# A half step's third weight sum in the raw ring, and the operand sums transposed ahead into two pairs of PSUM banks

## The chip, the cores and the metric

One core of one Trainium2 chip runs the whole program. The metric is the device time of one execution in microseconds (us), taken as the median of several runs; lower is better. TensorE is called PE here, its weight load PEld, VectorE DVE, ScalarE ACT, GpSimd POOL and the queue of SyncE, which issues the weight loads, SP.

## The reference

The kernel computes two transformer layers on one sequence of 512 tokens of width 1024 in fp32. Layer 0 mixes tokens by two kinds of attention, layer 1 by a pool mixer; behind each stands a feed-forward network. What matters for this change is that network and its sandwich norms (hidden width 2816 = 22 columns of 128, that is 11 column pairs):

```
h = h + rmsnorm(mixer(rmsnorm(h)))
u = rmsnorm(h)
h = h + rmsnorm((silu(u @ w_gate) * (u @ w_up)) @ w_down)
```

## The kernel before, in words

**Precision.** PE takes fp32r operands, so each fp32 matrix is split into a high part and a low part (hi, lo), and a product is three matmuls: hi·hi, hi·lo, lo·hi (`three` at L332 to L334, `prod` at L944 to L946). Weights come from HBM into a ring of raw tiles (`load_raw`, tag `wr`, 11 tiles of 128x512, DMAs on the SP queue); `conv` makes the high part on ACT (L244, tile `wh`) and the low part on DVE or POOL (L245, tile `wl`) in a second ring, `wq`, of 14 tiles, which are 7 hi/lo pairs.

**The feed-forward network.** `Ffn.run` computes gate and up of the 11 column pairs in 22 half steps. A half step is a 2x2 block product with seven block products in place of eight. Each has 4 x 3 = 12 matmuls of 256 columns: `begin` does the products of weights "11" and "s2" into a psA bank, `middle` "s3" and "s1" into a psS bank and then "12" into psA, `end` "22" and "s4" into psS. Two of the seven (p1 from "11" and "12") are already there for the column pairs that `front` computed ahead, so their half steps have five. The weight sums s1 to s4 of a half step are made on DVE by `comb` in `pair_weights` (L913): a half step loads four raw tiles (a11, a21, a22, a12), s3 = a11 - a21 goes into a tile of its own, and the other three sums overwrite raw tiles (a21, a11, a12). s3's tile comes from a ring of two tiles, tag `jk`, which it shares with the products `mq` of `post_norm` (L822). `put` then converts each block into hi and lo.

**The operand sums.** `combine` makes the four sums of blocks of the normed activations (tiles `tt`, L881, on DVE) and transposes each on PE, two times four 128x128 transposes per sum (`transpose_pair`, L311). Each group of four lands in one PSUM bank of tag psT, of which there are two; ACT takes the high part (L220, tile `th`), DVE the low part (L221, tile `tl`), and then the bank is free. `turn` transposes the normed activations themselves (tiles `un` into `uh` and `ul`) the same way. The tags psA, psS, psT and psO have two banks each.

**What sets the order.** A scheduler puts each engine's instructions in a fixed order when the kernel is built, by program order, priorities and its own estimate of time; `tc.high_priority(n)` puts its body ahead by n places. `conv` and `comb` run with n = `hpw` = 0. On the chip every engine works through its own list in order, so an instruction that has to wait holds all behind it. Between the attention or the pool mixer and `run` stand transition 1 (around 280 to 360 us) and transition 2 (640 to 740 us), whose program order is a string of steps: W and T are products of the projection before, N, E and F the norms, M the mixer, R `turn`, A `front`, Z `combine`. In both strings Z stands second to last, ahead of one A alone.

Of the kernel before, what the change touches and what calls it, by code (L numbers as in the profile page):

```python
# [6 lines left out]
F32 = mybir.dt.float32  # L7
# [6 lines left out]
P = 128  # L14
# [15 lines left out]
CFG = dict(  # L30
    order=ORDER,
    norm='vggvgvvg',
    wlo0='g',
    wlo1='ggv',
    ng=31,
    no=8,
    xe=4,
    pt=4,
    w=14,
    wr=11,  # L40
    jk=2,
    psb=(2, 2, 2, 2),
    early=('kc', 'vc'),
# [9 lines left out]
    hpa=200,  # L53
# [59 lines left out]
def trunk(ctx: ExitStack, tc, x, norm_g, w_in, b_f, cmp_pe, cmp_w1, cmp_w2, w_out,  # L113
# [9 lines left out]
    def nm(s):  # L123
        names[s] = names.get(s, 0) + 1
        return f"{s}_{names[s]}"

    def T(shape, tag, bufs, dt=F32, label=None):
        return sb.tile(shape, dt, tag=tag, bufs=bufs, name=nm(label or tag))
# [3 lines left out]
    def G(shape, dt=F32, label="g"):  # L132
        return T(shape, "g", CFG["ng"], dt, label)
# [7 lines left out]
    def JK(label, n=S, dt=F32):  # L141
        return T([P, n], "jk", CFG["jk"], dt, label)
# [13 lines left out]
    def BANK(tag, shape=(P, S)):  # L156
        return ps.tile(list(shape), F32, tag=tag, bufs=psb[tag], name=nm(tag))

    def r32(ap):
        return ap.bitcast(F32)  # L160
# [4 lines left out]
    def cols(w, c0, n, k0=0, nk=KC):  # L165
        return w[k0 * P:(k0 + nk) * P, c0:c0 + n].rearrange("(k p) f -> p k f", p=P)

    def load_raw(src, shape):

        n, w = shape[1:]  # L170
        m = max(1, min(n, 512 // w))
        raws = []
        for a in range(0, n, m):
            raw = T([P, m, w], "wr", CFG["wr"])
            nc.sync.dma_start(raw, src[:, a:a + m, :])
            raws.append(raw)
        return raws
# [41 lines left out]
    def split(dst_hi, dst_lo, src):  # L219
        nc.scalar.activation(dst_hi, src, AF.Copy)  # L220
        nc.vector.tensor_sub(dst_lo, src, r32(dst_hi))  # L221
# [4 lines left out]
    def WQ2(shape):  # L226
        return WQ(shape, "wh"), WQ(shape, "wl")
# [11 lines left out]
    def next_engine(key):  # L239
        return nc.vector if choose(key) == "v" else nc.gpsimd  # L240

    def conv(hi, lo, src, key="wlo"):
        with tc.high_priority(CFG["hpw"]):
            nc.scalar.activation(hi, src, AF.Copy)  # L244
            next_engine(key).tensor_tensor(lo, src, r32(hi), op=ALU.subtract)  # L245
# [60 lines left out]
    def transpose_pair(dst, srcs, ks, tag, gcol=None):  # L306

        pt = BANK(tag)
        for a, k in enumerate(ks):
            for j in range(2):  # L310
                nc.tensor.transpose(pt[:, a * 256 + j * P:a * 256 + (j + 1) * P], srcs[j][:, k * P:(k + 1) * P], ident)  # L311
        hi, lo = dst
        if gcol is None:
            split(hi, lo, pt.rearrange("p (k c) -> p k c", k=2))
            return
        for a, k in enumerate(ks):
            g = gT[:, gcol * 8 + k:gcol * 8 + k + 1]
            o = pt[:, a * 256:(a + 1) * 256]
            nc.scalar.activation(hi[:, a, :], o, AF.Copy, scale=g)
            nc.vector.scalar_tensor_tensor(lo[:, a, :], o, g, r32(hi[:, a, :]), op0=ALU.mult, op1=ALU.subtract)  # L320
# [4 lines left out]
    def transpose_half(u, uns, half, gcol=None, tags=("psT",), first=0):  # L325
        cs = slice(half * 256, (half + 1) * 256)
        for k2 in range(first, KC // 2):
            ks = slice(2 * k2, 2 * k2 + 2)
            transpose_pair((u[0][:, ks, cs], u[1][:, ks, cs]), uns, (2 * k2, 2 * k2 + 1), tags[k2 % len(tags)], gcol)
# [485 lines left out]
    def post_norm(t, bk, hs, g_bc, store=False):  # L815
        sq = SM([P, 2], "sq2")
        for n in range(2):
            nc.scalar.activation(trash[:, 0:S], bk[n], AF.Square, scale=1.0 / 32, accum_out=sq[:, n:n + 1])
        rs = rstd_of(sq)
        junk = [JK("mq") for _ in range(2)]  # L820
        for n in range(2):
            nc.vector.tensor_tensor(junk[n], bk[n], g_bc[n], op=ALU.mult)  # L822
        for n in range(2):
            cs = slice(n * S, (n + 1) * S)
            if choose("hup") == "v":
                nc.vector.scalar_tensor_tensor(hs[t][:, cs], junk[n], rs, hs[t][:, cs], op0=ALU.mult, op1=ALU.add)
            else:
                nc.scalar.activation(junk[n], junk[n], AF.Copy, scale=rs)
                nc.gpsimd.tensor_tensor(hs[t][:, cs], junk[n], hs[t][:, cs], op=ALU.add)
            if store:  # L830
                (nc.sync, nc.scalar)[n].dma_start(out[0, t * P:(t + 1) * P, cs], hs[t][:, cs])
# [4 lines left out]
    class Ffn:  # L836
# [14 lines left out]
            self.uns.append(norm_row(self.hs[t], self.g))  # L851

        def turn(self, half):
            transpose_half(self.u, self.uns[2 * half:2 * half + 2], half, first=2 * half)

        def front(self, p):
            a = [RAW(2 * p), RAW(2 * p + 1)]
# [14 lines left out]
        def combine(self):  # L872

            lo_, hi_ = slice(0, S), slice(S, D)
            ts = [[], [], [], []]
            for j in range(2):
                a, b = self.uns[j], self.uns[2 + j]
                t1, t2, t3, t4 = (G([P, S], label="tt") for _ in range(4))
                for o, x0, x1 in ((t1, b[:, lo_], a[:, lo_]), (t3, b[:, hi_], b[:, lo_]),
                                  (t2, b[:, hi_], t1), (t4, a[:, hi_], t2)):  # L880
                    next_engine("sadd").tensor_tensor(o, x0, x1, op=ALU.subtract)  # L881
                for m, t_ in enumerate((t1, t2, t3, t4)):
                    ts[m].append(t_)
            self.T = {}
            for n_, m in enumerate((0, 2, 3, 1)):
                his, los = [], []
                for k2 in range(2):
                    hi, lo = (G([P, 2, 256], F32R, label=l_) for l_ in ("th", "tl"))
                    transpose_pair((hi, lo), ts[m], (2 * k2, 2 * k2 + 1), "psT")
                    his += [hi[:, k, :] for k in range(2)]  # L890
                    los += [lo[:, k, :] for k in range(2)]
                self.T[m + 1] = (his, los)
# [4 lines left out]
        def pair_weights(self, w_, p):  # L897


            def block(r, j):  # L900
                return load_raw(cols(w_, (2 * p + r) * P, P, 4 * j, 4), [P, 4, P])[0]

            a11, a21, a22, a12 = block(0, 0), block(1, 0), block(1, 1), block(0, 1)
            W = {}

            def put(name, src):
                hi, lo = WQ2([P, 4, P])
                conv(hi, lo, src, "slo")
                W[name] = ([hi[:, k, :] for k in range(4)], [lo[:, k, :] for k in range(4)])

            def comb(o, x0, x1, op):
                with tc.high_priority(CFG["hpw"]):
                    next_engine("sadd").tensor_tensor(o, x0, x1, op=op)  # L913

            s3 = JK("s3").rearrange("p (k c) -> p k c", k=4)
            if p not in self.ws:
                put("11", a11)
            comb(s3, a11, a21, ALU.subtract)
            comb(a21, a21, a22, ALU.add)
            comb(a11, a21, a11, ALU.subtract)  # L920
            put("s2", a11)
            yield W
            put("s3", s3)
            put("s1", a21)
            if p not in self.ws:
                put("12", a12)
            comb(a12, a12, a11, ALU.subtract)
            yield W
            put("22", a22)
            put("s4", a12)  # L930
            yield W
# [104 lines left out]
    f0 = Ffn(0, hs, G)  # L1036
# [12 lines left out]
        return  # L1049
    bk = {}  # L1050

    def post_feed(t):
        post_norm(t, bk[t], hs, g_bc)
        f0.feed(t)

    steps = {
        "T": lambda t: bk.__setitem__(t, tail(t)),
        "W": f0.weights,
        "N": post_feed,
        "R": f0.turn,  # L1060
        "A": f0.front,
        "Z": f0.combine,
    }
    for step in CFG["tr1"].split():
        steps[step[0]](*(int(c) for c in step[1:]))
# [2 lines left out]
    class Pool:  # L1068
# [82 lines left out]
    f1 = Ffn(1, hs, G)  # L1151
# [7 lines left out]
        "F": f1.feed,  # L1159
        "R": f1.turn,  # L1160
        "A": f1.front,
        "Z": f1.combine,
    }
    for step in CFG["tr2"].split():
        steps[step[0]](*(int(c) for c in step[1:]))
# [34 lines left out]
```

## Time and profile before

| what | value |
|---|---|
| median of 3 runs | 1073.12 us (1072.94 to 1074.51) |
| the profiled execution, its own time | 1071.16 us |
| its span, first to last instruction | 1069.4 us |
| mean granted clock of PE | 0.987 of 2.4 GHz |
| busy: PE, DVE, ACT, POOL | 96%, 71%, 53%, 29% of the span |
| HBM | 102 MB read, 97 GB/s over the span |

An engine's busy share is its time in instructions over the span. The granted clock is told as a share of full speed; a stretch at 0.52 is one at the lower of the two levels for nearly all of its time. Names such as `psT L311 <- DVE tl L221` say that the instruction of line 311 that writes psT waited for the instruction of line 221 on DVE that writes tl.

### The profile page before, as it was taken

The numbers are of one execution on the slowest core, as the hardware profiler recorded it, in microseconds if no ns is written. First come the engines' busy times: TensorE is split into PE (matmuls) and PEld (weight loads), VectorE is DVE, ScalarE is ACT, GpSimd is POOL, SyncE is SP. The second block draws the span as 40 slices with busy tenths as digits, with TensorE's granted clock in tenths as the row PEclk, the third lists the DMA queues.
The fourth block names the chain that finished last, engine by engine and source line by source line (L and its number), as shares of the span: only waits on it lengthen the run. The fifth ranks groups of instructions, "written<-read, shape, count | busy, mean of one in ns | idle before, by whom it ended". The sixth has DMA issues, their size and how long they took to land.

```text
span 1069.4 us, 19004 instructions
## 1 busy us (share of the span) xinstructions
PE 1023.3 (96%) x6892; PEld 940.4 (88%) x6892; DVE 755.3 (71%) x1527; ACT 563.0 (53%) x1194; POOL 314.5 (29%) x282
## 2 busy tenths in 40 slices
PE   6999999997999999999999999988999999999997
PEld 5788978896888999999988888988999999978886
DVE  5338898758749999899973153998898898881204
ACT  6437688769656454454564352764444354472401
POOL 5713666767751000000026371420000000053510
PEclk9999999999999999999999999998999999999999
DMA  8841201323531434433343374003342333433302
GB/s 244 195 96 40 60 21 32 95 73 102 169 89 31 119 109 116 123 102 107 119 153 114 106 218 110 21 11 92 97 138 83 112 114 90 139 117 121 108 1 78
DMA packets 156493, 108.58 MB, mean 102 GB/s; under 512 B 14836, under 2 KB 137584, under 8 KB 156400
## 3 DMA queue, kind: packets, MB, share of 16 engines
q1 hardware_dynamic: 155600, 106.23, 34.6%
q8 instruction: 54, 0.88, 0.4%
q10 hardware_dynamic: 800, 1.15, 0.3%
q14 instruction: 39, 0.32, 0.1%
HBM read 101.88 MB, written 2.10 MB: 97 GB/s over the span
## 4 chain that ended last, share of the span: by engine, by line
PE 77%; DVE 8%; ACT 5%; issue 3%; DMA 3%; POOL 2%; SPq 1%; DVEq 0%; POOLq 0%; ACTq 0%
PE psS L944 8%; PE psS L945 8%; PE psS L946 7%; PE psA L944 5%; PE psA L945 5%; PE psA L946 5%; PE psT L784 2%; PE psO L784 2%; PE psT L782 2%; PE psT L783 2%; PE psO L783 2%; PE psO L782 2%; PE psA L782 2%; PE psA L784 2%; PE psA L783 2%
## 5 line engine op out<-in xcount | busy, mean ns | idle before, releaser
L244 ACT ACTIVATE wh<-wr 128x512 fp32r<-128x512 f32 x376 | 226.3, 626 | 256.8 <-DVE wr L913 82.4
L245 POOL TENSOR_TENSOR wl<-wr,wh 128x512 fp32r<-128x512 f32 x101 | 145.4, 1449 | 556.5 <-ACT wh L244 329.8
L245 DVE TENSOR_TENSOR wl<-wr,wh 128x512 fp32r<-128x512 f32 x275 | 189.5, 706 | 92.1 <-ACT wh L244 89.4
L944 PE MATMUL psS<-th,wh 128*128 128x256 f32 x528 | 149.8, 285 | 1.3 <-DVE comb L964 1.3
L945 PE MATMUL psS<-tl,wh 128*128 128x256 f32 x528 | 150.0, 285 | 0.0
L946 PE MATMUL psS<-th,wl 128*128 128x256 f32 x528 | 149.9, 284 | 0.0
L944 PEld LDWEIGHTS psS<-th,wh 128*128 128x128 f32 x528 | 101.6, 193 | 1.6 <-DVE comb L964 0.9
L945 PEld LDWEIGHTS psS<-tl,wh 128*128 128x128 f32 x528 | 101.8, 193 | 0.0
L946 PEld LDWEIGHTS psS<-th,wl 128*128 128x128 f32 x528 | 101.7, 193 | 0.0
L913 DVE TENSOR_TENSOR wr<-wr,wr 128x512 f32<-128x512 f32 x132 | 86.7, 682 | 1.3 <-DMA wr<-in_ffn_w_up_dram 0.5
L946 PE MATMUL psA<-uh,wl 128*128 128x256 f32 x272 | 77.5, 286 | 3.1 <-DVE wl L245 3.0
L944 PE MATMUL psA<-uh,wh 128*128 128x256 f32 x272 | 77.5, 286 | 2.1 <-DVE comb L962 1.7
L945 PE MATMUL psA<-ul,wh 128*128 128x256 f32 x272 | 77.3, 284 | 0.0
L270 POOL TENSOR_SCALAR E<-E,ri 128x128 f32<-128x128 f32 (+3 forms) x48 | 56.0, 1167 | 38.8 <-DVE ri L590 12.9
L584 ACT ACTIVATE E<-E,mn 128x128 f32<-128x128 f32 (+1 forms) x96 | 53.4, 557 | 15.7 <-DVE mn L582 15.0
L946 PEld LDWEIGHTS psA<-uh,wl 128*128 128x128 f32 x272 | 52.6, 194 | 3.5 <-DVE wl L245 3.5
L944 PEld LDWEIGHTS psA<-uh,wh 128*128 128x128 f32 x272 | 52.5, 193 | 2.7 <-DVE comb L962 2.1
L332 PE MATMUL psA<-uh,wh 128*128 128x512 f32 (+1 forms) x136 | 51.4, 378 | 1.7 <-DVE nq L464 1.5
L945 PEld LDWEIGHTS psA<-ul,wh 128*128 128x128 f32 x272 | 52.6, 193 | 0.0
L221 DVE TENSOR_TENSOR pl<-psT,ph 128x512 fp32r<-128x512 f32 (+1 forms) x72 | 42.3, 593 | 12.5 <-ACT ph L220 8.7
L334 PE MATMUL psA<-uh,wl 128*128 128x512 f32 (+1 forms) x136 | 50.9, 374 | 0.0
L333 PE MATMUL psA<-ul,wh 128*128 128x512 f32 (+1 forms) x136 | 50.7, 373 | 0.0
(354 smaller groups left out, 3009.8 us busy)
## 6 DMA issues: line engine op xcount, KB each, us to landing
wr<-in_ffn_w_gate_dram SPq DMA_DIRECT2D x98, 256.0 KB
wr<-in_ffn_w_up_dram SPq DMA_DIRECT2D x98, 256.0 KB
wr<-in_ffn_w_down_dram SPq DMA_DIRECT2D x88, 256.0 KB
wr<-in_attn_w_in_dram SPq DMA_DIRECT2D x40, 256.0 KB
wr<-in_attn_w_out_dram SPq DMA_DIRECT2D x16, 256.0 KB
x<-in_x_dram SPq DMA_DIRECT2D x4, 512.0 KB
gbc<-in_norm_g_dram SPq DMA_DIRECT2D x8, 256.0 KB
h<-in_x_dram SPq DMA_DIRECT2D x4, 512.0 KB
```

The source lines that it names most:

```text
L244: nc.scalar.activation(hi, src, AF.Copy)
L245: next_engine(key).tensor_tensor(lo, src, r32(hi), op=ALU.subtract)
L270: (nc.vector if k == "v" else nc.gpsimd).tensor_scalar(e, e, s1, None, op0=ALU.mult)
L332: nc.tensor.matmul(psum, wh, ah, start=first, stop=False)
L584: nc.scalar.activation(e, e, AF.Exp, bias=mn[:, n_:n_ + 1], scale=-1.0, accum_out=sm[:, n_:n_ + 1])
L782: nc.tensor.matmul(o, acts[c][0][:, tok], wh[k], start=first, stop=False)
L783: nc.tensor.matmul(o, acts[c][0][:, tok], wl[k], start=False, stop=False)
L784: nc.tensor.matmul(o, acts[c][1][:, tok], wh[k], start=False, stop=last)
L913: next_engine("sadd").tensor_tensor(o, x0, x1, op=op)
L944: nc.tensor.matmul(o, wh, bh, start=start and k == 0, stop=False, skip_group_check=True)
L945: nc.tensor.matmul(o, wh, bl, start=False, stop=False, skip_group_check=True)
L946: nc.tensor.matmul(o, wl, bh, start=False, stop=k == 3, skip_group_check=True)
```

## The change

Four edits. The raw ring gets a twelfth tile. The sum s3 takes its tile from that ring and no more from `jk`. `turn` of the second half, and `combine`, put their groups of four transposes into psT and psO banks in turn. And `combine` runs with a priority 200 places ahead (`hpa` = 200) in both transitions.

```
-    wr=11,
+    wr=12,
...
         def turn(self, half):
-            transpose_half(self.u, self.uns[2 * half:2 * half + 2], half, first=2 * half)
+            transpose_half(self.u, self.uns[2 * half:2 * half + 2], half, first=2 * half, tags=("psT", "psO") if half else ("psT",))
...
-                    transpose_pair((hi, lo), ts[m], (2 * k2, 2 * k2 + 1), "psT")
+                    transpose_pair((hi, lo), ts[m], (2 * k2, 2 * k2 + 1), ("psT", "psO")[k2])
...
-            s3 = JK("s3").rearrange("p (k c) -> p k c", k=4)
+            s3 = T([P, 4, P], "wr", CFG["wr"], F32, "s3")
...
+    def ahead(f):
+        def g():
+            with tc.high_priority(CFG["hpa"]):
+                f()
+        return g
+
...
-        "Z": f0.combine,
+        "Z": ahead(f0.combine),
...
-        "Z": f1.combine,
+        "Z": ahead(f1.combine),
```

The built order moves with it. On DVE in transition 2, between the last residual of `post_norm` (L826) and the sums `tt` of `combine`: s_23 and s_24 are the s3 tiles of the first two half steps of layer 1, the `wr` rows of L913 their second and third sums.

```order
-L913 TENSOR_TENSOR s_23_8925<-wr_8917,wr_8919 128x512
 L221 TENSOR_TENSOR ul_8056<-psT_8632,uh_8055 128x2x256
-L913 TENSOR_TENSOR s_24_8958<-wr_8950,wr_8952 128x512
-L913 TENSOR_TENSOR wr_8919<-wr_8919,wr_8921 128x512
 L279 TENSOR_SCALAR ms_8750<-ssq_8748 128x1
-L913 TENSOR_TENSOR wr_8952<-wr_8952,wr_8954 128x512
 L881 TENSOR_TENSOR tt_8771<-un_8736,un_8467 128x512
-L913 TENSOR_TENSOR wr_8917<-wr_8919,wr_8917 128x512
+L297 SCALAR_TENSOR_TENSOR un_8747<-h_3612,rs_8752,g_4_8059 128x512
```

These five rows now stand far ahead, among the last conversions of the pool mixer's weights, in front of the first norm of the mixer's output (ms L277); so do two conversions of the first half step (wl_8934 and wl_8938). Later on the same engine, around the first evictions of the half steps (`comb` L962, on which PE's product of "12" waits), still in transition 2:

```order
 L245 TENSOR_TENSOR wl_8983<-wr_8952,wh_8982 128x512
-L221 TENSOR_TENSOR tl_8842<-psT_8843,th_8841 128x512
-L913 TENSOR_TENSOR wr_9185<-wr_9187,wr_9185 128x512
-L221 TENSOR_TENSOR tl_8851<-psT_8852,th_8850 128x512
-L245 TENSOR_TENSOR wl_8987<-wr_8956,wh_8986 128x512
-L913 TENSOR_TENSOR wr_9191<-wr_9191,wr_9185 128x512
-L913 TENSOR_TENSOR wr_8956<-wr_8956,wr_8950 128x512
-L245 TENSOR_TENSOR wl_9071<-wr_9058,wh_9070 128x512
 L962 TENSOR_TENSOR comb_8993<-psA_8991,comb_8993 128x256
 L962 TENSOR_TENSOR comb_9093<-psA_9091,comb_9093 128x256
+L245 TENSOR_TENSOR wl_8987<-wr_8956,wh_8986 128x512
```

The two `tl` rows have moved up, and seven sums and conversions of the third and fourth half step that stood in front of L962 (five of them here) now stand behind it. On PE, the first transposes of the last `turn` (un) and of `combine` (tt) in transition 2, among the products of `front` (psA_8861, psS_8888):

```order
+L311 MATMUL psT_8757<-cst,un_8736 128x128
+L311 MATMUL psO_8764<-cst,un_8736 128x128
+L311 MATMUL psT_8789<-cst,tt_8771 128x128
+L311 MATMUL psO_8798<-cst,tt_8771 128x128
+L334 MATMUL psA_8861<-uh_8055,wl_8332 128x256
+L332 MATMUL psS_8888<-uh_8055,wh_8339 128x256
+L333 MATMUL psS_8888<-ul_8056,wh_8339 128x256
+L334 MATMUL psS_8888<-uh_8055,wl_8340 128x256
+L311 MATMUL psT_8757<-cst,un_8747 128x128
```

Before, the transposes of `tt` came behind the products of `front` and the first two of `begin`, sixteen in a row and all in psT; now they stand in smaller groups between those products, in psT and psO by turns. Transition 1 moves in the same way on both engines.

## Rows read from the trace of the kernel before

**Rows 1.** The page, busy time of each engine: us (share), instructions.
```profile
PE 1023.3 (96%) x6892; PEld 940.4 (88%) x6892; DVE 755.3 (71%) x1527; ACT 563.0 (53%) x1194; POOL 314.5 (29%) x282
```

**Rows 2.** Windows: length, busy us (count) by engine, PE clock, DMA share, GB/s.
```profile
340.00:360.00 20.00, 15.98 (x125) 14.53 (x124) 19.06 (x34) 10.73 (x20) 0.00 (x0) 1.00 0.28 79
360.00:380.00 20.00, 20.00 (x169) 20.00 (x168) 17.50 (x35) 9.76 (x17) 0.00 (x0) 1.00 0.39 109
...
420.00:440.00 20.00, 20.00 (x169) 20.00 (x168) 19.45 (x36) 10.60 (x20) 0.00 (x0) 1.00 0.52 145
...
700.00:718.50 18.50, 15.46 (x129) 15.05 (x127) 18.50 (x35) 11.79 (x25) 6.58 (x6) 0.98 0.05 13
718.50:732.20 13.70, 10.59 (x48) 9.49 (x49) 11.01 (x21) 5.57 (x11) 0.00 (x0) 0.52 0.21 62
```

**Rows 3.** Timeline of PE, transition 1: start, length, instruction, idle before and its releaser.
```profile
341.04 0.36 PE L944 MATMUL psA<-uh,wh 128*128 128x256 f32 x1 [0.39 <-DVE act L868]
...
344.29 0.65 PE L311 MATMUL psT<-cst,tt 128*128 128x128 f32 x4 [0.55 <-DVE tl L221]
...
346.42 0.66 PE L311 MATMUL psT<-cst,tt 128*128 128x128 f32 x4 [1.36 <-DVE tl L221]
...
348.22 0.66 PE L311 MATMUL psT<-cst,tt 128*128 128x128 f32 x4 [0.43 <-DVE tl L221]
...
358.69 0.38 PE L944 MATMUL psA<-uh,wh 128*128 128x256 f32 x1 [1.17 <-DVE comb L962]
```

**Rows 4.** Timeline of PE, transition 2.
```profile
718.59 0.58 PE L946 MATMUL psA<-uh,wl 128*128 128x256 f32 x1 [3.04 <-DVE wl L245]
...
724.07 2.32 PE L311 MATMUL psT<-cst,tt 128*128 128x128 f32 x8 [1.26 <-DVE tl L221]
...
728.28 1.12 PE L311 MATMUL psT<-cst,tt 128*128 128x128 f32 x4 [1.68 <-DVE tl L221]
...
740.77 0.39 PE L944 MATMUL psA<-uh,wh 128*128 128x256 f32 x1 [0.51 <-DVE comb L962]
```

**Rows 5.** Timeline of DVE, transition 2.
```profile
704.53 1.72 DVE L913 TENSOR_TENSOR s<-wr,wr 128x512 f32<-128x512 f32 x1
...
707.38 0.68 DVE L913 TENSOR_TENSOR wr<-wr,wr 128x512 f32<-128x512 f32 x1
707.98 0.14 DVE L279 TENSOR_SCALAR ms<-ssq 128x1 f32<-128x1 f32 x1
...
710.45 0.74 DVE L297 SCALAR_TENSOR_TENSOR un<-h,rs,g 128x512 f32<-128x512 f32 x1
...
717.86 0.68 DVE L245 TENSOR_TENSOR wl<-wr,wh 128x512 fp32r<-128x512 f32 x1
...
723.34 0.68 DVE L221 TENSOR_TENSOR tl<-psT,th 128x512 fp32r<-128x512 f32 x1
...
732.20 0.69 DVE L221 TENSOR_TENSOR tl<-psT,th 128x512 fp32r<-128x512 f32 x1 [1.45 <-ACT th L220]
```

**Rows 6.** Timeline of DVE, ahead of the two transitions.
```profile
296.61 0.69 DVE L822 TENSOR_TENSOR mq<-psT,gbc 128x512 f32<-128x512 f32 x1 [3.15 <-ACT trash L818]
...
326.44 2.38 DVE L913 TENSOR_TENSOR s<-wr,wr 128x512 f32<-128x512 f32 x2
...
658.05 0.21 DVE L277 TENSOR_SCALAR ms<-sq 128x1 f32<-128x1 f32 x1 [10.48 <-ACT trash L818]
```

**Rows 7.** Timeline of PE in layer 0's attention.
```profile
249.92 0.41 PE L577 MATMUL psS<-fkA,fqA 128*128 128x384 f32 x1 [3.08 <-DMA fkA<-fkA]
```

**Rows 8.** Window of 3.5 us behind that wait, columns as in rows 2.
```profile
249.90:253.40 3.50, 3.48 (x13) 3.16 (x14) 2.69 (x10) 3.35 (x9) 2.68 (x4) 0.56 0.27 81
```

**Rows 9.** Waits: engine, line, releaser: us in total, times, longest us.
```profile
DVE s L913 <- DMA wr<-in_ffn_w_gate_dram: 8.9, 10, 2.3
...
PEld psT L311 <- DVE tl L221: 7.4, 7, 2.0
```

## The prediction

> **What bounds the kernel now.** I read the busy times first, then windows of 20 us, then the PE timeline wherever a window shows less than 20 us of PE. PE is busy for 96% of the span [rows 1], so the change can only win time where PE stands still or runs slowly. In the steady half steps there is nothing to win: PE is busy 20.00 of 20 us with 169 matmuls [rows 2], 0.118 us each, so a half step of 84 matmuls takes 9.9 us, while DVE is busy 17.5 to 19.45 of 20. DVE is there the second engine, with a slack of 0.55 to 2.5 us in 20. The exceptions are the transitions. In 340 to 360 us PE loses 4.02 us at a full clock. From 700 to 718.5 it loses 3.04 and from 718.5 to 732.2 another 3.11, and in that last stretch the granted clock is 0.52, the lower of the two levels nearly throughout. DVE is busy 19.06 of 20 and 18.50 of 18.50 just there: in the transitions DVE is the bound and PE waits for it.
>
> The PE timeline says for what. In transition 1 [rows 3] it waits 0.55, 1.36 and 0.43 us for a psT bank that `tl` has not yet emptied, and 1.17 for the eviction L962; with 0.39 for an activation of `front` that is 3.90. In transition 2 [rows 4] it waits 3.04 for a low half of a weight (`wl`), 1.26 and 1.68 for psT banks and 0.51 for L962: 6.49. The slow clock there costs more: 10.59 us of work at 0.52 are 5.5 us of work at full speed, so 5.1 are lost. Together 11.6 in transition 2 and 3.9 in transition 1, 15.5 us in all. That is what lies within reach.
>
> **The change, part by part.**
>
> *s3 out of `jk`.* In the `jk` ring s3 stood behind the `mq` tiles of the norm, so the first weight sums could not start before the norm's last `mq` was used. That is why they sit at 704.53 in transition 2 [rows 5] and at 326.44 in transition 1 [rows 6]. With a tile of their own kind they move, in the built order, into stretches where DVE idles: 3.15 us before its first `mq` of transition 1 and 10.48 before the norm in transition 2 [rows 6]. Their own time costs nothing there, as DVE has that idle time and PE does not wait for it. What leaves the crowded stretch of transition 2 is five sums and two conversions: the first took 1.65 us (704.53 to the next row), the others 0.60 from start to start (707.38 to 707.98), so 1.65 + 6 x 0.60 = 5.25 us.
>
> What that frees: the statistic `ms` of the last norm tile stood at 707.98 behind three of those sums [rows 5], 2.85 us of them, and the `un` made from it at 710.45. It comes at most 2.85 us earlier; its input from ACT is late too, and I take 2.1. The `wl` on which PE waits 3.04 starts at 717.86. By the list alone it would start at 717.86 - 5.25 - 0.60 (s_25, also moved behind) + 3 x 0.60 (two `ul` and one `tt` now in front), 713.8. But the two `ul` need transposes that PE issues between products of `front`, so I put it at 716.8, which leaves some 0.8 of the 3.04. The ends are 0 and 3.04.
>
> *Two pairs of banks and Z ahead.* The transposes of `combine` now have four banks to run into and stand between products in smaller groups, and the `tl` rows stand further ahead on DVE. My walk through DVE's new list has the first `tl` at 720.2 in place of 723.34 [rows 5], 3.2 us earlier. Seven sums and conversions of later half steps moved from before L962 to behind it, 7 x 0.60 = 4.2 us. So L962 and the product of "12" behind it come 3.2 + 4.2 = 7.4 us earlier: 733.4 in place of 740.77 [rows 4]. Counted on PE it is the same: of the 11.6 us lost, some 4.2 stay, 0.8 for `wl`, the rest in shorter waits for `th` and `tl` (the wait of `tl` on ACT is as long as 1.45 at 732.20, and ACT's part does not get shorter). This presumes that the clock holds at those shorter waits, as it did in transition 1, where 2.34 us of waits within some 4 us left it at 1.00 [rows 2, 3]. No transposes are added, so the banks cost nothing on PE; a psO bank is free once the norm before has read it, before the first group.
>
> Does the second pair of banks bring anything by itself? The rows say that PE waited 2.34 us in transition 1 and 2.94 in transition 2 for just that, 5.3 us, and the list of waits has 7.4 us of weight loads that waited on `tl` [rows 9]. The Trainium skill speaks against it: the page "TensorE: Matmul & The Clock Gate", section "HAM oscillation — how this bites in real kernels", tells of a kernel for which more PSUM buffers gave no further gain (126.6 to 125.5 us). By that page the sum would be some -5.6. I go by the rows: these waits end at an eviction, and DVE's part of them shrinks too.
>
> In transition 1 the same moves take s and sums out of 326.44 onward (a row of 2.38 us for the two s), and the same 4.2 us from before L962. The 3.90 us of waits are shorter than what is freed, so nearly all go; the 0.39 for the activation of `front` I leave. I take -3.5; the ends are 0 and -3.9.
>
> *What is deferred.* The 4.2 us put behind L962 come back in the first half steps, where DVE has 2.5 us to spare in 360 to 380 [rows 2]. The `wq` ring holds the weights of one half step, so what those 2.5 do not take in may return as a wait on `wl` soon after: 0 to 4.2 - 2.5 = 1.7 us per transition. I take 0, since the moved rows belong to half steps three and four.
>
> *The raw ring.* A half step took 4 of 11 tiles and takes 5 of 12, so the ring holds 2.4 half steps in place of 2.75: loads start up to 0.35 x 9.9 = 3.5 us nearer to their use. Today DVE waits 8.9 us in ten places for gate loads [rows 9], none longer than 2.3, and PE feels next to nothing of it. In the new order a tile of s3 is handed on soon after its conversion, and the fewest DVE instructions between the release of a tile and the first use of what is loaded into it is 12 where it was 5. So I take 0, between -1.2 and what the rival below says. In layer 0 a twelfth tile lets each load start one tile sooner, in nearly the old order: 0, with bounds of one clock stretch lost or won, like the 3.5 us at 0.56 behind a wait of 3.08 [rows 7, 8], which is 1.5 us either way.
>
> **Sum.** -3.5 - 7.4 + 0 + 0 = -10.9 us. The profiled execution's own time was 1071.16, so it would become 1060.3; that run lies 2.0 below the median shown, and against the median the prediction is 1073.12 - 10.9 = **1062.2**.
>
> **The rivals.**
>
> *B, the clock falls again.* Waits of some 4 us stay bunched around 716 to 728. If the clock falls for as long as before, 5.1 us of the gain are lost: -5.8, **1067.3**. For it: before the fall PE had lost 3.04 us at one piece, and the 3.08 at 249.92 was followed by a clock of 0.56 too [rows 4, 7, 8]. Against: no single wait stays near 3 us in the walk. Chance 0.16.
>
> *F, the second pair of banks brings nothing.* ACT's `th` and DVE's `tl` take what they take, so a PE that runs four groups ahead only waits at the products instead, on `th` and `tl`: the 5.3 us stay, -10.9 + 5.3 = -5.6, **1067.5**. For it: `tl` waits for ACT too, 1.45 us at 732.20 [rows 5]. Against: the walk with 7.4 us counts DVE's rows alone, and these get fewer. Chance 0.08. The Trainium skill's sentence above is this rival's.
>
> *C, PE never waits there.* DVE and ACT get so far ahead that all 15.5 us go: **1057.6**. Against it: the last norm tile still ends a chain ACT, DVE, POOL, DVE, PE that PE cannot cover. Chance 0.07.
>
> *D, DVE only moves the debt.* DVE's total work does not change, and it is 97% busy in some steady windows as well (19.45 of 20 [rows 2]). If the 5.25 and the 4.2 us come back as `wl` waits in the next half steps, and PE's waits in the transition move rather than go, the change does not do what it says: **1073** within 0.2%, that is 2.1 us, which is about what a measurement of this kernel can tell from no change. Against: 2.5 us in 20 are free behind transition 1, and the 5.25 us truly go into idle time. Chance 0.08.
>
> *E, the raw ring runs dry, slower.* The third sum holds a raw tile from the sum to its conversion on ACT and DVE. If that is long, the loads of the second half step ahead start late, and DVE, working in order, stands in front of L913 with evictions queued behind. DVE has about 0.3 to 1.2 us of slack in a half step [rows 2]; from the point where a half step's load comes later than that, PE waits for the rest. An excess of 1 us in about half of the 44 half steps is +22, with the 10.9 gained **1084**. For it: ten waits for loads exist already, up to 2.3 us long, and the lead shrinks by up to 3.5 us. Against: the count of instructions between release and use, which grows. Chance 0.09.
>
> The forecast, 1060 to 1065, has what is left, 0.52. Faster by over 0.2% are the forecast, B, F and C: 0.83; within 0.2% is D: 0.08; slower is E: 0.09. The range goes from C, 1057.5, past B and F, with up to 2.5 of returned work on top of these, to 1070.0; it leaves out D and E and a little of C, 2 in 10.
>
> **What would show it.** Right: PE's window of 340 to 360 at 19.5 or more; the clock between 700 and 735 at 1.00; no `wl` wait over 1 us before the second half step; the waits of L311 on `tl` below 2 us in all; s of the first two half steps in the idle stretches ahead of the norms; the first product of "12" of transition 2 some 11 us earlier than before, 7.4 of it won there. Wrong: a clock near 0.5 again after 715 (B); PE windows in the steady half steps below 20.00, with waits on `wl` just behind the transitions (D), or on L913 and loads all along both networks (E); PE waits that merely change their releaser from `tl` to `th` or `tt`.

## The result, and the profile after

The changed kernel took 1056.28 us (median of 4 runs, 1055.17 to 1058.51) against 1073.03 beside it: a ratio of 0.9858, 95% interval 0.9839 to 0.9877. In a second comparison (e9 below) it was 1058.54 against 1071.11, ratio 0.9881, interval 0.9857 to 0.9905. It is 1.2% to 1.4% faster. 1062.2 was forecast, with a range of 1057.5 to 1070.0. The first median lies 1.2 us below that range and the second inside it. The gain is near the price of rival C, but it is not C that happened: PE still waits in transition 2, as the rows below show.

Windows of the changed kernel, with the columns of [rows 2]; the last row goes from the steady weight products ahead of transition 1 to 2 us before the first wait of the second down projection:

```profile
340.00:360.00 20.00, 19.54 (x164) 19.34 (x163) 20.00 (x38) 10.94 (x20) 0.00 (x0) 1.00 0.37 106
...
700.00:720.00 20.00, 18.47 (x153) 17.59 (x151) 18.91 (x35) 14.53 (x30) 0.96 (x2) 1.00 0.09 26
720.00:740.00 20.00, 19.73 (x164) 19.73 (x165) 20.00 (x38) 8.47 (x14) 0.00 (x0) 1.00 0.51 146
...
300.00:924.24 624.24, 617.23 (x4609) 590.55 (x4608) 508.65 (x899) 321.00 (x592) 97.42 (x78) 1.00 0.36 106
```

In 340 to 360 PE lost 4.02 us [rows 2] and now loses 0.46, all of it in one wait:

```profile
353.10 0.39 PE L944 MATMUL psS<-th,wh 128*128 128x256 f32 x1 [0.46 <-DVE comb L964]
```

In transition 2, where 3.04 and 3.11 us were idle and the clock stood at 0.52 for 13.7 us, it now loses 1.53 and 0.27 and the clock stays at 1.00. DVE is as full as before (20.00 of 20): it does the same work, in an order that lets PE go on.

The PE timeline of the changed kernel in transition 2, every idle stretch over 0.2 us between 700 and 740, where [rows 4] had 6.49 us:

```profile
713.33 0.66 PE L311 MATMUL psT<-cst,tt 128*128 128x128 f32 x4 [0.50 <-DVE tl L221]
...
714.53 0.66 PE L311 MATMUL psO<-cst,tt 128*128 128x128 f32 x4 [0.54 <-DVE tl L221]
...
715.47 0.66 PE L311 MATMUL psT<-cst,tt 128*128 128x128 f32 x4 [0.28 <-DVE tl L221]
...
720.27 0.39 PE L945 MATMUL psA<-tl,wh 128*128 128x256 f32 x1 [0.48 <-DVE tl L221]
```

The timeline of DVE, against [rows 5, 6]:

```profile
292.50 0.69 DVE L913 TENSOR_TENSOR s<-wr,wr 128x512 f32<-128x512 f32 x1 [3.80 <-DMA wr<-in_ffn_w_gate_dram]
...
643.99 0.69 DVE L913 TENSOR_TENSOR s<-wr,wr 128x512 f32<-128x512 f32 x1 [4.74 <-DMA wr<-in_ffn_w_up_dram]
...
651.89 0.21 DVE L277 TENSOR_SCALAR ms<-sq 128x1 f32<-128x1 f32 x1 [3.01 <-ACT trash L818]
...
700.07 0.15 DVE L279 TENSOR_SCALAR ms<-ssq 128x1 f32<-128x1 f32 x1 [0.46 <-ACT trash L286]
...
701.85 0.74 DVE L297 SCALAR_TENSOR_TENSOR un<-h,rs,g 128x512 f32<-128x512 f32 x1
...
709.86 0.68 DVE L245 TENSOR_TENSOR wl<-wr,wh 128x512 fp32r<-128x512 f32 x1
...
712.60 0.68 DVE L221 TENSOR_TENSOR tl<-psT,th 128x512 fp32r<-128x512 f32 x1
```

The first sums now run where DVE has nothing else to do, at 292.50 and 643.99, and even wait there for their loads (3.80 and 4.74 us) without PE waiting for them. To compare the later rows with [rows 5], 6.1 us must be taken off first: the first down projection, whose first product waits 1.17 us in both kernels, stands at 553.08 before and at 546.97 after:

```profile
553.08 0.50 PE L782 MATMUL psT<-wh,ah 128*128 128x512 f32 x1 [1.17 <-ACT ah L220]
```

```profile
546.97 0.50 PE L782 MATMUL psT<-wh,ah 128*128 128x512 f32 x1 [1.17 <-ACT ah L220]
```

Against that, `ms` is 1.8 us earlier, `un` 2.5, the `wl` 1.9 and the first `tl` 4.6.

**A measure without the attention stage.** Executions of one kernel differ by several us here (the kernel before took 1066.89 to 1075.22 over all comparisons). Much of it lies ahead of 300 us: the clock falls there for 3.4 us at a time (for 6.8 us once each in e1 and e6), at about 43, 60, 91, 251 and 268 us, in the profiles told of here at none to five of these places. So beside each ratio stands PE's loss from 300 us to 2 us ahead of the second down projection: the length of that stretch less PE's busy time, plus half of PE's busy time where the clock is at its lower level. After: 624.24 - 617.23 = 7.0. Before, from the same window of the kernel before,

```profile
300.00:940.64 640.64, 625.97 (x4622) 597.18 (x4621) 508.66 (x902) 316.10 (x592) 98.44 (x78) 0.99 0.36 104
```

640.64 - 625.97 = 14.7, plus half of the 10.59 in the slow stretch of [rows 2], 5.3, is 20.0. The change wins **13.0** there. The windows of the slow stretches take in a little of the full clock (0.52 to 0.59 is granted in them, not 0.50), so the part for the slow clock is an estimate and up to 0.4 us too high. Ahead of 300 us, from PE's first instruction near 6 us, the same sum was 22.9 before and 20.4 in the first profile of the change; e9 shows what that is worth.

### The profile page after: what moved, and what is told of

Read it like the earlier page. It is cut to its first block, busy times and chain, and to the rows that moved or that the text cites. A ratio compares the mean times of both kernels' runs of the same rounds, so it can differ in the third digit from the quotient of the medians.

```text
span 1053.0 us, 19039 instructions
## 1 busy us (share of the span) xinstructions
PE 1015.3 (96%) x6892; PEld 934.6 (89%) x6892; DVE 757.9 (72%) x1527; ACT 568.3 (54%) x1194; POOL 319.5 (30%) x282
## 4 chain that ended last, share of the span: by engine, by line
PE 58%; DVE 3%; issue 1%; ACT 1%; POOL 0%; DMA 0%; DVEq 0%; POOLq 0%; ACTq 0%
PE psS L946 7%; PE psS L944 7%; PE psS L945 7%; PE psA L944 5%; PE psA L945 5%; PE psA L946 4%; PE psT L784 2%; PE psA L783 2%; PE psA L782 2%; PE psO L784 2%; PE psA L784 2%; PE psO L783 2%; PE psT L783 2%; PE psT L782 2%; PE psO L782 2%; PE psS L782 2%
## 5 line engine op out<-in xcount | busy, mean ns | idle before, releaser
L244 ACT ACTIVATE wh<-wr 128x512 fp32r<-128x512 f32 x376 | 230.4, 628 | 265.9 <-DVE wr L913 73.0
L245 POOL TENSOR_TENSOR wl<-wr,wh 128x512 fp32r<-128x512 f32 x101 | 151.6, 1509 | 539.8 <-ACT wh L244 539.2
L245 DVE TENSOR_TENSOR wl<-wr,wh 128x512 fp32r<-128x512 f32 x275 | 194.0, 718 | 88.0 <-ACT wh L244 86.5
L913 DVE TENSOR_TENSOR wr<-wr,wr 128x512 f32<-128x512 f32 x132 | 88.1, 685 | 1.0 <-DMA wr<-in_ffn_w_up_dram 0.2
L584 ACT ACTIVATE E<-E,mn 128x128 f32<-128x128 f32 (+1 forms) x96 | 53.4, 557 | 13.6 <-DVE mn L582 13.1
L944 PE MATMUL psA<-th,wh 128*128 128x256 f32 x176 | 50.0, 285 | 1.8 <-ACT comb L954 1.8
```

The lines of the kernel that those rows point to most:

```text
L584: nc.scalar.activation(e, e, AF.Exp, bias=mn[:, n_:n_ + 1], scale=-1.0, accum_out=sm[:, n_:n_ + 1])
L944: nc.tensor.matmul(o, wh, bh, start=start and k == 0, stop=False, skip_group_check=True)
```

## The experiments

| kernel | ratio to before (95%) | idle + slow clock = loss from 300 us, us |
|---|---|---|
| before | 1 | 14.7 + 5.3 = 20.0 |
| the change; e9, the same again | 0.9858; 0.9881 (0.9857 to 0.9905) | 7.0; 7.0 |
| e1, s3 alone | 0.9932 (0.9911 to 0.9953) | 10.3 + 3.4 = 13.7 |
| e2, banks alone | 0.9938 (0.9919 to 0.9958) | 10.6 + 1.7 = 12.3 |
| e3, not ahead | 0.9891 (0.9851 to 0.9931) | 7.0 |
| e4, e10, 11 raw tiles | 0.9875 (0.9837 to 0.9913); 0.9857 (0.9830 to 0.9884) | 6.0; 5.9 |
| e5, `jk` of three | 0.9950 (0.9933 to 0.9967) | 13.4 + 2.9 = 16.3 |
| e6, own tile | 0.9883 (0.9848 to 0.9918) | 7.1 |
| e7, sums twice | 0.9963 (0.9945 to 0.9981) | 13.7 + 4.9 = 18.6 |
| e8, turn in psT | 0.9885 (0.9852 to 0.9918) | 8.6 |
| e11, 10 raw, 16 wq | 0.9840 (0.9812 to 0.9867) | 6.3 |
| e12, 9 raw tiles | 0.9898 (0.9867 to 0.9930) | 6.6 + 3.4 = 10.0 |

**e1, s3 alone.** From the kernel before:

```
-    wr=11,
+    wr=12,
-            s3 = JK("s3").rearrange("p (k c) -> p k c", k=4)
+            s3 = T([P, 4, P], "wr", CFG["wr"], F32, "s3")
```

> s3 in the raw ring of 12 and nothing else: the transposes stay in psT alone, Z is not put ahead. Theory (both parts are needed, and they add up through the clock): the weight sums leave the transitions, so the 3.04 us wait on wl in transition 2 goes and the clock holds there (5.1 us), but the waits of the transposes on tl stay, some 5.3 us of the change's 16.7: about 1061.5, with L311 waits on tl of 4 to 6 us. Rival (the second pair of banks brings nothing): 1056 to 1058, with those waits gone too. Rival (the banks are the whole gain): 1071 to 1073, the clock near 0.5 in transition 2 again.

Measured 1064.53, between the theory's 1061.5 and the 1071 of the second rival: 6.3 us less loss than before. The `wl` wait is gone, the bank waits are there, and the clock fell behind them after all. The PE timeline and the window of its slow stretch:

```profile
718.22 0.66 PE L311 MATMUL psT<-cst,tt 128*128 128x128 f32 x4 [1.28 <-DVE tl L221]
...
719.42 0.66 PE L311 MATMUL psT<-cst,tt 128*128 128x128 f32 x4 [0.54 <-DVE tl L221]
...
722.16 0.69 PE L311 MATMUL psT<-cst,tt 128*128 128x128 f32 x2 [1.97 <-DVE tl L221]
```

```profile
722.30:729.10 6.80, 6.80 (x36) 6.80 (x37) 4.28 (x7) 2.28 (x4) 0.00 (x0) 0.57 0.30 87
```

So 3.79 us of bank waits stay in transition 2 without the second pair of banks. They and the clock at 0.57 for 6.8 us make up most of what the whole change does better there.

**e2, banks alone.** From the kernel before:

```
-            transpose_half(self.u, self.uns[2 * half:2 * half + 2], half, first=2 * half)
+            transpose_half(self.u, self.uns[2 * half:2 * half + 2], half, first=2 * half, tags=("psT", "psO") if half else ("psT",))
-                    transpose_pair((hi, lo), ts[m], (2 * k2, 2 * k2 + 1), "psT")
+                    transpose_pair((hi, lo), ts[m], (2 * k2, 2 * k2 + 1), ("psT", "psO")[k2])
```

> Transposes into psT and psO in turn and nothing else: s3 stays in the ring it shares with mq, 11 raw tiles, Z not ahead. Theory: the sums of the first half steps still crowd DVE around 704 to 718 us, so the wait on wl of some 3 us stays in transition 2 and the clock falls there; only the 5.3 us of waits on tl go: about 1067.5. Rival (banks are the whole gain): 1056 to 1058 and the clock at 1.00 around 720. Rival (banks bring nothing): 1072 to 1073.

Measured 1064.37, 7.7 us less loss: somewhat more than the theory gave. The `wl` wait stays, as it said; the clock falls later and for 3.4 us only:

```profile
714.63 0.38 PE L946 MATMUL psA<-uh,wl 128*128 128x256 f32 x1 [2.18 <-DVE wl L245]
...
716.76 0.66 PE L311 MATMUL psO<-cst,tt 128*128 128x128 f32 x4 [0.25 <-DVE ul L221]
...
718.02 0.38 PE L944 MATMUL psS<-th,wh 128*128 128x256 f32 x1 [0.60 <-ACT th L220]
...
720.11 0.69 PE L311 MATMUL psT<-cst,tt 128*128 128x128 f32 x2 [1.70 <-DVE tl L221]
```

Rival F, that the second pair brings nothing, falls here: 0.9938 with an interval that ends at 0.9958. The sentence of the Trainium skill ("TensorE: Matmul & The Clock Gate", "HAM oscillation — how this bites in real kernels") on PSUM buffers without further gain is told of another kernel and is not borne out in this one. s3 alone is worth 6.3 and the banks alone 7.7; together 14.0, against 13.0 measured. The two parts nearly add.

**e3, not ahead.** From the change:

```
-        "Z": ahead(f0.combine),
+        "Z": f0.combine,
-        "Z": ahead(f1.combine),
+        "Z": f1.combine,
```

> The whole change without the priority of Z. In the built order only ten lines of PE's list differ from the change's, and none on the other engines. Theory: priority does nothing here, 1056.3 within 2 us. Rival (putting Z ahead is what shortens the transitions): 1060 or more, with waits of L311 on tl of 3 us or more.

The loss from 300 us on is the change's, 7.0, with the same four waits in transition 2. The median (1059.73 of 4) is higher than the 1056.3 within 2 us that was expected, but the interval of its ratio takes in 0.9858. By the loss the priority does nothing; without it the transposes stand ahead in the order all the same, so the other parts moved them.

**e4 and e10, 11 raw tiles.** From the change:

```
-    wr=12,
+    wr=11,
```

> The whole change with 11 raw tiles in place of 12, so a half step takes 5 of 11 (2.2 half steps ahead). Theory (the lead of the loads is not what limits, DVE's slack takes in their waits): 1056 to 1059. Rival (the raw ring is near its limit): DVE waits for loads at L913 in many half steps, over 20 us in all, PE waits behind them, 1063 or more.

> The change with 11 raw tiles once more. Its loss from 300 us on was 1.1 us less than the change's (5.95 against 7.02). Theory (the twelfth tile brings nothing, s3's place and the banks are all of it): the same as the change's run beside it within 1.5 us, perhaps 1 us faster. Rival (the twelfth tile is needed): 2 us or more slower than the change.

1057.59 (ratio 0.9875), and 1055.58 beside the change's 1058.54, with a loss of 6.0 and 5.9 us. The twelfth tile is not needed. In transition 2 two of the change's four waits remain, at 0.49 and 0.28; in the steady half steps three waits on `wl` of 0.8 us stand where the change has three on ACT (below).

**e5, a third tile in `jk`.** From the change:

```
-    wr=12,
-    jk=2,
+    wr=11,
+    jk=3,
-            s3 = T([P, 4, P], "wr", CFG["wr"], F32, "s3")
+            s3 = JK("s3").rearrange("p (k c) -> p k c", k=4)
```

> The change with the twelfth tile given to the ring that s3 shares with mq (three tiles there), and s3 left in it; 11 raw tiles; transposes in psT and psO in turn, Z ahead. Theory (s3 was late because it stood behind mq in one ring): the first sums still stand behind the norm's last mq in DVE's list, so this is worth no more than the banks alone, 1064 to 1066, with the waits on wl of some 2 us in transition 2. Rival (s3 only lacked a tile, whichever ring has it): 1056 to 1059.

1066.46, near the theory's 1064 to 1066, and even 4 us more loss than the banks alone. With the same memory but in the ring of `mq`, the first sums stay behind the norm. The place of the main wait differs from what was expected: not `wl`, but one wait of 4.83 us for a `tl`, followed by a stretch at 0.54:

```profile
724.81 0.69 PE L311 MATMUL psT<-cst,tt 128*128 128x128 f32 x2 [4.83 <-DVE tl L221]
```

So it is not the tile that counts, but in which order its ring is handed on.

**e6, a tile of its own.** From the change:

```
-    wr=12,
+    wr=11,
-            s3 = T([P, 4, P], "wr", CFG["wr"], F32, "s3")
+            s3 = T([P, 4, P], "s3r", 1, F32, "s3")
```

> The change with a tile of s3's own (a ring of one) beside 11 raw tiles, so that a half step takes 4 of 11 raw tiles as before. Theory (what counts is that s3 no longer waits for mq, whoever owns the tile): 1055 to 1059, the wait on wl in transition 2 under 0.5 us. Rival (s3 needs several tiles, so that two half steps' sums can be made in the idle stretches): only the first half step's sums go ahead, 1060 to 1063, with waits of matmuls on wl in the steady half steps as well.

1059.66, between the theory's range and the rival's, with a loss of 7.1: by the loss equal to the change, for the theory. The rival is half right: three of the steady half steps of layer 0 wait 0.65 to 0.88 us on `wl`, as in this row, while from 330 to 360 us, in transition 1, no wait over 0.2 us is left:

```profile
368.99 0.39 PE L946 MATMUL psA<-th,wl 128*128 128x256 f32 x1 [0.88 <-DVE wl L245]
```

**e7, sums twice.** From the change (in layer 1 each L881 is issued a second time):

```
-                    next_engine("sadd").tensor_tensor(o, x0, x1, op=ALU.subtract)
+                    for _ in range(1 + self.layer):
+                        next_engine("sadd").tensor_tensor(o, x0, x1, op=ALU.subtract)
```

> The change, with each of the eight operand sums of transition 2 (L881) done twice by DVE: 8 x 0.60 = 4.8 us more on DVE between 700 and 712 us, the values are the same. Theory (DVE's own list sets the pace of transition 2): PE waits for most of it, the stretch from transition 2 to the second down is 3 to 5 us longer, and if the clock falls again 2 to 5 more: 1060 to 1066. Rival (PE's chain through ACT and POOL sets it, DVE has room): less than 1 us, 1056 to 1058.

1068.36, past the upper end: 4.8 us of DVE work cost 11.6 us of loss. The two long waits of PE stand below, and at the end of the first of them the clock falls for the same 13.7 us as in the kernel before:

```profile
715.12 0.90 PE L311 MATMUL psT<-cst,tt 128*128 128x128 f32 x3 [3.42 <-DVE tt L882]
...
721.74 0.48 PE L311 MATMUL psT<-cst,tt 128*128 128x128 f32 x1 [3.80 <-DVE tl L221]
```

```profile
715.10:728.80 13.70, 9.88 (x48) 9.18 (x49) 11.82 (x20) 5.81 (x10) 0.00 (x0) 0.53 0.14 39
```

DVE's list sets the pace of transition 2, and a microsecond on it costs more than one.

**e8, turn in psT.** From the change:

```
-            transpose_half(self.u, self.uns[2 * half:2 * half + 2], half, first=2 * half, tags=("psT", "psO") if half else ("psT",))
+            transpose_half(self.u, self.uns[2 * half:2 * half + 2], half, first=2 * half)
```

> The change, with the second half's turn left in psT alone; the operand sums of combine still alternate. Theory (the waits that mattered were those of combine's sixteen groups, turn has two groups that two banks hold): 1056 to 1058.5. Rival (turn's groups in psT block combine's first ones): 1059 or more, with a wait of L311 on ul of 1 us or more in transition 2.

1059.42 and a loss of 8.6, 1.6 more than the change: the rival's number, not its place. No wait on `ul` appears; transition 1 has one wait of 1.43 us on `tl` (at 348.18) and transition 2 two, of 0.88 and 0.48. The ratios do not tell the two kernels apart (e9: 0.9881), so `turn`'s share is at most these 1.6 us.

**e9, the change again.**

> The change itself once more, beside the next three on one chip. Theory (from 300 us on PE loses 7.0 us in place of 19.9, the rest of the first difference, some 2 to 3 us, was the clock in the attention stage, which falls at other times in each execution): ratio 0.986 to 0.989, and the loss from 300 us on within 0.3 us of 7.0 whatever the clock does ahead of it. Rival (the change also holds the clock in the attention stage): 0.985 or less, with no more than two falls of the clock ahead of 300 us.

0.9881, and a loss from 300 us on of 7.0, as in the first profile:

```profile
300.00:928.69 628.69, 621.64 (x4628) 594.25 (x4627) 509.83 (x903) 321.52 (x592) 97.61 (x78) 1.00 0.37 107
```

This profile has four falls of the clock ahead of 300 us and a loss there of 25.2, more than the 22.9 of the kernel before. So the 2.5 us by which the first profile of the change was better there are not the change's.

**e11, 10 raw tiles and 16 of wq.** From the change:

```
-    w=14,
-    wr=12,
+    w=16,
+    wr=10,
```

> The change with 10 raw tiles and 16 tiles of hi and lo weights in place of 12 and 14: the memory of the two raw tiles goes to one more pair of converted weights. Theory (what is left behind 300 us, waits on wl and on ACT of 0.2 to 0.8 us in steady half steps, comes from weights converted just in time): a pair more takes them away, 1 to 2 us faster than the change. Rival (2.0 half steps of raw tiles are too few): DVE waits for loads at L913 and PE loses more than 9 us from 300 us on, slower than the change by 2 us or more.

1053.66 beside the change's 1058.54, ratio 0.9840: the lowest median of the kernels run, and lower than the change's by more than the theory gave, though the intervals of the two ratios still overlap a little. But the place was not the expected one: from 300 us on it loses 6.3, only 0.7 less, and the steady half steps of layer 0 still wait 0.24 us on ACT and two times 0.65 on `wl`. The rest is ahead of 300 us: two falls of the clock against four in e9, and an idle time of 14.5 us against 17.0 and 18.3 in the two profiles of the change. Two waits on loads in the attention stage, first in the changed kernel:

```profile
59.81 0.30 PE L400 MATMUL psS<-BL,w 128*64 128x62 f32 x2 [2.70 <-DMA w<-in_nsa_cmp_w_dram]
...
248.67 0.41 PE L577 MATMUL psS<-fkA,fqA 128*128 128x384 f32 x1 [2.69 <-DMA fkA<-fkA]
```

In e11 the first is gone and the second is a shorter one on ACT:

```profile
247.39 0.41 PE L577 MATMUL psS<-fkA,fqA 128*128 128x384 f32 x1 [0.92 <-ACT OT L647]
```

For the first wait e12 tells more: with 9 raw tiles and `wq` as in the change, L400 runs there without a wait as well, while all kernels here with 11 or 12 raw tiles wait 2.2 to 3.8 us at that place. So it goes with the raw tiles and not with `wq`. That fewer raw tiles put fewer weight loads ahead of these small ones would explain it, but is not shown. The second wait stays in e12 in another form (3.83 us for `fqA` from DVE); why e11 has it shorter is open.

**e12, 9 raw tiles.** From the change: `wr=9` in place of 12.

> The change with 9 raw tiles, 1.8 half steps of 5: a test of the rival E, that the raw ring runs dry. Theory (the lead has room to spare, DVE's slack takes in the waits): within 3 us of the change. Rival E: waits for loads in most of the 44 half steps, PE loses 15 us or more from 300 us on, and the kernel is slower than 1066.

1060.15, within 3 us of the change, with a loss of 10.0. Rival E falls: DVE waits at L913 for loads in four places, not in most half steps. The ring does get tighter: ACT's conversions (L244) wait 13.6 us for gate loads in five places, where the changed kernel has no such wait, but PE's idle time, 6.6 us, shows nothing of it. Of the 10.0, 3.4 are a fall of the clock in the pool mixer (last section).

## Why the prediction was right, and what it mis-sized

**What bounds the kernel.** Right. Of the 15.5 us of PE waits and slow clock that it found the change took 13.2, and PE now loses 7.0 us in all from 300 us on. e7 shows the bound directly, in transition 2 of the changed kernel.

**Transition 1, -3.5.** Right there: the 3.90 us of [rows 3] became one wait of 0.46 at 353.10 (shown above). But "deferred: I take 0" was wrong by 1.6 us, inside its bounds of 0 to 1.7 and in another form. Not `wl` comes late but ACT's copy of p1 (L954), three times, on a PE that had no waits there before:

```profile
383.08 0.39 PE L944 MATMUL psA<-th,wh 128*128 128x256 f32 x1 [0.69 <-ACT comb L954]
...
418.13 0.39 PE L944 MATMUL psA<-th,wh 128*128 128x256 f32 x1 [0.24 <-ACT comb L954]
...
453.63 0.39 PE L944 MATMUL psA<-th,wh 128*128 128x256 f32 x1 [0.68 <-ACT comb L954]
```

ACT's timeline ahead of the first of them has, in front of the copy, a conversion that waits until PE has given back a weight tile; PE's last product ahead of its wait stands below it:

```profile
382.13 0.63 ACT L244 ACTIVATE wh<-wr 128x512 fp32r<-128x512 f32 x1 [0.81 <-PE psA L945]
382.66 0.36 ACT L954 ACTIVATE comb<-psA 128x256 f32<-128x256 f32 x1
```

```profile
382.12 0.28 PE L945 MATMUL psS<-tl,wh 128*128 128x256 f32 x1
```

The conversion alone is not the cause, for the kernel before has the same pair on ACT with the same 0.81 us, and its PE does not wait:

```profile
390.59 0.63 ACT L244 ACTIVATE wh<-wr 128x512 fp32r<-128x512 f32 x1 [0.81 <-PE psA L945]
391.13 0.37 ACT L954 ACTIVATE comb<-psA 128x256 f32<-128x256 f32 x1
```

```profile
392.14 0.28 PE L944 MATMUL psA<-th,wh 128*128 128x256 f32 x1
```

What differs is PE's order. There, 14 products into psS stand between the last one of p1 and the product that waits for the copy (the one at 392.14); now only two do, at all three places. At 418.13 no conversion is in the way, and PE waits 0.24 us for the copy itself. So these 1.6 us come with PE's new order; that the sums that DVE deferred cause them is not shown.

**Transition 2, -7.4.** The mechanism was right, the term too small: of 11.6 us lost, 1.8 stay, so 9.8 went. The first product of "12", which was to come 7.4 us earlier, comes 9.1 earlier (at 725.52 in place of 740.77, less the 6.1). The step that failed is "some 4.2 stay", and in it the sentence that "ACT's part does not get shorter". The wait of `tl` on ACT (1.45 at 732.20 in [rows 5]) was taken for ACT's own time. The timeline of ACT in the kernel before shows ACT itself waiting, for transposes that PE issued late for want of a bank and, from 718.5 to 732.2, at half the clock:

```profile
729.43 0.60 ACT L220 ACTIVATE th<-psT 128x512 fp32r<-128x512 f32 x1 [2.41 <-PE psT L311]
731.56 0.60 ACT L220 ACTIVATE th<-psT 128x512 fp32r<-128x512 f32 x1 [1.54 <-PE psT L311]
```

It was a ring PE, ACT, DVE, bank, PE, and it went with the banks: these waits of ACT add up to 7.0 us before, 6.5 with s3 alone (e1), 3.4 with the banks alone (e2) and 1.3 in the changed kernel, while ACT's own work on `th` in transition 2 takes 4.66 us before and 4.57 after. In the list of waits of the kernel before and of the changed one:

```profile
ACT th L220 <- PE psT L311: 7.0, 8, 2.4
```

```profile
ACT th L220 <- PE psO L311: 0.9, 3, 0.6
...
ACT th L220 <- PE psT L311: 0.4, 1, 0.4
```

The links ahead of that held: `ms` 1.8 us earlier (2.1 taken), the first `tl` 4.6 (3.2 taken). Of the `wl` wait 0.8 was to stay and none did: its `wl` is ready at 710.5, and PE, which has more transposes to do in front of it, asks for it only at 711.29, which without the 6.1 is 1.9 us later than before. The 0.8 did not follow from the prediction's own 716.8 either: a `wl` that starts 1.06 us earlier leaves 2.0 of the 3.04, unless PE asks later, which the prediction did not say.

```profile
711.29 0.36 PE L946 MATMUL psA<-uh,wl 128*128 128x256 f32 x1
```

**The clock.** That it holds in transition 2 was right, and necessary for the sum. Rival B was real all the same: with either part alone (e1, e2) it falls for 6.8 or 3.4 us.

**The banks.** The prediction gave the waits on `tl` 5.3 us by the rows; e2 gives 7.7 with what the clock adds.

**The raw ring, 0.** Right. Waits of the s3 sums for loads were 12.6 us in 18 places (8.9 in ten of them [rows 9]) and are 11.0 in 4, two of them the long ones in idle stretches shown above:

```profile
DVE s L913 <- DMA wr<-in_ffn_w_up_dram: 7.2, 3, 4.7
...
DVE s L913 <- DMA wr<-in_ffn_w_gate_dram: 3.8, 1, 3.8
```

With 11, 10 and 9 tiles PE's idle time from 300 us on shows nothing of rival E. It priced the ring by tiles per half step, and not by how soon a tile is handed on; that this is why it failed is argued here, not measured.

**Not foreseen.** The waits of 0.53 and 0.72 us on L964 late in layer 1 are gone too, near the bound of -1.2 that the prediction gave and did not take.

**Sum.** -10.9 predicted, -13.0 in the stages that the change touches: -3.4 in transition 1, -9.8 in transition 2, -1.2 on L964, +1.6 on L954, and small rests. The medians say -16.8 and -12.6. The first of them has luck in it: its profiled executions differ by 2.5 us in the attention stage, which e9 does not repeat. That is more than the 1.2 by which 1056.28 lies below the range.

## What to carry to other kernels

A temporary that shares a ring with tiles of a later stage inherits their place in the order: giving it another ring was worth 6 us here, a third tile in the same ring nothing. When an engine waits for an eviction that waits for a third engine, look at what that third one waits for before counting its time as a floor; it may be the first engine, a bank short. And where the clock falls at PE's waits, a microsecond on the engine that PE waits for can cost two or more: 4.8 us cost 11.6 in e7.

## What the runs showed of the hardware

The granted clock also fell, to the lower of its two levels, at places where each of PE's waits was short. In e12 it fell at 676.9 us, in the pool mixer, for 6.8 us, behind three waits of 0.41 to 0.44 us within 4.5 us; the last two of them and the window:

```profile
674.05 0.33 PE L1132 MATMUL psA<-band,vl 128*128 128x128 f32 x1 [0.44 <-DVE vl L1109]
...
676.03 0.33 PE L1132 MATMUL psO<-band,vl 128*128 128x128 f32 x1 [0.42 <-DVE vl L1109]
```

```profile
660.00:680.00 20.00, 18.73 (x99) 16.25 (x98) 15.98 (x25) 11.29 (x26) 6.84 (x8) 0.92 0.05 14
```

In transition 1 of the kernel before, 2.34 us of waits within 4.5 us left it at 1.00 [rows 2, 3]. And one kernel loses it at other places from execution to execution: the two profiles of the change show falls at 90 and 250 us, and at 62, 92, 253 and 270 us. Each fall of 3.4 us costs up to 1.7, half of PE's work in it, and so the total time of this kernel moves by several us, more than some of the parts measured here; only the stage by stage count tells these apart.
